# Low parts of the output weights made twice, rows kept on chip through the MLP, sums spread, casts ahead

## The chip, the core and the metric

The kernel runs on one core of one Trainium2 chip. The metric is the device time of one execution in microseconds (us), the median of three runs. In what follows PE is the matrix engine, VectorE is DVE in the views, ScalarE is ACT, GpSimd is POOL, and SP is the engine that issues most transfers.

## What is computed

One layer on 2048 rows of 1024 features: a mixer, a cross attention to 256 memory tokens, and an MLP, each added to the running rows `h`.

```python
h = h + jnp.concatenate([y_pool, y_dn], axis=-1) @ w_out[l]
m = rmsnorm(mem, mem_norm_g[l])
h = h + memory_cross_attention(rmsnorm(h, norm_xattn_g[l]), m, w_xq[l], w_xk[l], w_xv[l], w_xo[l])
h = h + sqrelu_mlp(rmsnorm(h, norm_mlp_g[l]), w_up[l], w_down[l])
return rmsnorm(h, final_norm_g)          # sqrelu: relu(h w_up) squared, times w_down
```

The result of `rmsnorm` is a row times one factor r = 1/sqrt(mean(h^2) + eps) times a gain. The squared relu makes r come out of the MLP as r^2.

## The kernel before

After a prologue (the mixer and the memory's keys and values, up to about 873 us) the rest is 22 products of 1024 x 1024 blocks, called macros here and numbered 0 to 21. Macros 0 and 1 are the output projection (`o`) of the first and the second half of the rows (`sb` 0 and 1), 2 and 3 the scores (`s`), 4 and 5 the values (`v`), and 6 to 21 are up (`u`) and down (`d`) of the MLP in four groups of columns, the first half in 6 to 13, the second in 14 to 21.

A macro is done with seven block products instead of eight, its steps idx 0 to 6. Each step is 48 matmuls of 128 x 512 on PE (line 1003): each operand is split in a high part (cast by ScalarE, `sh`, `th`) and a low part (what is left, by VectorE, `sl`, `tl`), and three of the four products are taken. `S` is the operand with rows, `T` the weight side. Both need sums and differences of blocks: `adds` makes those of `S`, and `sums` makes those of `T` in eight units per matrix, each fetched by two transfers on GpSimd's queue into a tile `cb_...`, worked on by four additions (lines 161 to 164) on VectorE up to macro 6 and on GpSimd after it, and stored to `sums_...` by a transfer on GpSimd's queue. SP's queue loads them later as `t`.

In the first half's `o`, `s` and `v` macros each low part `tl` is also stored to `lo_o`, `lo_s`, `lo_v`, and the second half loads it from there on GpSimd's queue (line 929, in `prep`) instead of making it again.

The rows `or`, `sr`, `vr`, `dr` take the results: VectorE adds each 128 x 512 result to them (line 1037; for scores line 1055 with the row maximum, then exponentials on ScalarE, line 1066, and the scaling, lines 1071 and 1075). The first half's rows lie in eight tiles of the pool `h`, the second half's in eight of the ten of the pool `a`. `squares` takes the sums of squares and stores rows to `h_d`; after `v` it also scales the rows by r in place (line 1102), so that `turned` can transpose them on PE (line 1115, 64 transposes per macro, in steps 0, 2 and 3 of macros 1 to 6). The down macro's rows `dr` are loaded again from `h_d`.

PE's order is written out by hand throughout. For steps up to the end of macro 6 so are those of ScalarE, VectorE and GpSimd (`step_fixed`); from macro 7 on (`step_free`) a scheduler sets those. Each engine and each queue works in order: what waits holds all that is behind it.

## Time and profile before

| | |
|---|---|
| median of three runs | 2756.51 us (2750.58 to 2762.46) |
| the profiled execution | 2760.52 us |
| its span | 2758.6 us |
| PE busy | 2581.2 us, 94% of the span |
| VectorE busy | 1946.4 us, 71% |
| ScalarE busy | 1383.2 us, 50% |
| GpSimd busy | 836.3 us, 30% |
| moved by DMA | 518.65 MB |

[...]

### The profile page before, as it was taken

What the parts mean: (1) busy time and instruction counts of PE and PEld (TensorE: products, weight loads), DVE (VectorE), ACT (ScalarE), POOL (GpSimd) and SP (SyncE); (2) the same over time, 40 slices, a digit from 0 to 9 for tenths busy, and PEclk for the clock granted to TensorE, in tenths of its full rate; (3) what the DMA queues carried; (4) which work ended last, traced back from release to release, by engine and by line L of the source; (5) the groups of instructions that cost most, each with busy time, mean ns of one, the idle gap of its engine ahead of it and who ended that gap; (6) DMA issues with size and microseconds to landing.
All of it is one profiled execution on the core that took longest, in us unless ns stands there. A gap on an engine that the chain in (4) does not pass through costs nothing.

```text
span 2758.6 us, 35256 instructions
## 1 busy us (share of the span) xinstructions
PE 2581.2 (94%) x12822; PEld 2163.5 (78%) x12822; DVE 1946.4 (71%) x2531; ACT 1383.2 (50%) x2290; POOL 836.3 (30%) x881
## 2 busy tenths in 40 slices
PE   7999999999998987988997889999999999999998
PEld 6887788789787766776785678788888788888887
DVE  6865776765775766667657687888768685767666
ACT  6436535635534344675444435445464645545463
POOL 4333454431432222000012377887111202021100
PEclk9999999999999999999998999999999999999999
DMA  4335255244238999767998866656344634333232
GB/s 141 93 104 189 69 176 184 76 123 138 72 108 271 380 383 333 277 229 275 357 336 305 287 212 225 220 186 242 107 153 142 225 99 144 108 120 132 92 99 107
DMA packets 257080, 518.65 MB, mean 188 GB/s; under 512 B 36150, under 2 KB 106379, under 8 KB 256907
## 3 DMA queue, kind: packets, MB, share of 16 engines
q1 hardware_dynamic: 192858, 397.90, 42.8%
q0 software_dynamic: 28064, 97.53, 10.2%
q10 hardware_dynamic: 35984, 20.98, 2.7%
q8 instruction: 100, 1.64, 0.2%
q14 instruction: 74, 0.60, 0.1%
HBM read 383.17 MB, written 133.17 MB: 187 GB/s over the span
## 4 chain that ended last, share of the span: by engine, by line
PE 49%; DVE 12%; DMA 8%; issue 7%; ACT 5%; POOL 2%; SPq 0%; DVEq 0%; POOLq 0%; ACTq 0%
PE A L1003 23%; PE B L1003 17%; DVE tl L91 2%; DMA sums_v<-cb_v 2%; DVE sl L91 1%; DMA sums_w<-cb_w 1%; DMA or<-in_x_dram 1%; PE pcm L98 1%; PE pcm L99 1%; PE pcm L97 1%; ACT sh L90 1%; DVE cac L379 1%; ACT sr L1066 1%; PE px L492 1%; DMA t<-in_w_out_dram 1%
## 5 line engine op out<-in xcount | busy, mean ns | idle before, releaser
L1003 PE MATMUL A<-tl,sh 128*128 128x512 f32 x1392 | 549.0, 394 | 24.3 <-DMA tl<-lo_o 20.6
L1003 PE MATMUL A<-th,sh 128*128 128x512 f32 x1392 | 551.9, 396 | 12.4 <-DVE dr L1037 8.8
L1003 PE MATMUL A<-th,sl 128*128 128x512 f32 x1392 | 547.5, 393 | 0.0
L1003 PE MATMUL B<-tl,sh 128*128 128x512 f32 x1056 | 418.7, 397 | 26.3 <-DVE tl L91 9.3
L1003 PE MATMUL B<-th,sh 128*128 128x512 f32 x1056 | 418.4, 396 | 22.2 <-DVE nrs L1127 7.9
L1003 PE MATMUL B<-th,sl 128*128 128x512 f32 x1056 | 416.8, 395 | 0.0
L91 DVE TENSOR_TENSOR tl<-t,th 128x1024 fp32r<-128x1024 f32 x264 | 379.4, 1437 | 3.8 <-ACT th L90 3.6
L91 DVE TENSOR_TENSOR sl<-x,sh 128x1024 fp32r<-128x1024 f32 x166 | 225.5, 1359 | 184.4 <-ACT sh L90 184.0
L1003 PEld LDWEIGHTS A<-tl,sh 128*128 128x128 f32 x1392 | 265.2, 191 | 82.6 <-DMA tl<-lo_o 21.4
L1003 PEld LDWEIGHTS A<-th,sh 128*128 128x128 f32 x1392 | 265.1, 190 | 68.4 <-issue 9.6
L1003 PEld LDWEIGHTS A<-th,sl 128*128 128x128 f32 x1392 | 264.7, 190 | 55.5
L90 ACT CAST th<-t 128x1024 fp32r<-128x1024 f32 x264 | 275.7, 1044 | 36.2 <-DMA t<-sums_w 16.9
L90 ACT CAST sh<-x 128x1024 fp32r<-128x1024 f32 x166 | 173.8, 1047 | 221.1 <-PE B L1003 110.8
L1003 PEld LDWEIGHTS B<-tl,sh 128*128 128x128 f32 x1056 | 202.1, 191 | 73.5 <-DVE tl L91 12.7
L1003 PEld LDWEIGHTS B<-th,sh 128*128 128x128 f32 x1056 | 202.2, 191 | 66.4 <-ACT th L90 8.6
L1003 PEld LDWEIGHTS B<-th,sl 128*128 128x128 f32 x1056 | 202.0, 191 | 42.1
L90 ACT CAST sh<-c 128x1024 fp32r<-128x1024 f32 x96 | 100.3, 1045 | 218.8 <-PE A L1003 115.4
L97 PE MATMUL pcm<-hhi_x,wh_in 128*128 128x512 f32 x512 | 208.2, 407 | 0.2 <-ACT wh_in L90 0.2
L99 PE MATMUL pcm<-hhi_x,wl_in 128*128 128x512 f32 x512 | 205.1, 402 | 2.3 <-DVE wl_in L91 2.3
L98 PE MATMUL pcm<-hlo_x,wh_in 128*128 128x512 f32 x512 | 204.3, 399 | 0.0
L91 DVE TENSOR_TENSOR sl<-c,sh 128x1024 fp32r<-128x1024 f32 x96 | 126.8, 1321 | 65.4 <-ACT sh L90 65.4
L379 DVE SCALAR_TENSOR_TENSOR cac<-raw,vec,cac 128x512 f32<-128x512 f32 x144 | 129.3, 898 | 2.3
(359 smaller groups left out, 4720.8 us busy)
## 6 DMA issues: line engine op xcount, KB each, us to landing
ws_in<-in_w_in_dram SPq DMA_DIRECT2D x72, 512.0 KB, 3.8
x<-in_w_up_dram SPq DMA_DIRECT2D x64, 512.0 KB, 5.4
t<-sums_n SPq DMA_DIRECT2D x64, 512.0 KB, 4.5
t<-sums_w SPq DMA_DIRECT2D x64, 512.0 KB, 3.3
t<-n_d SPq DMA_DIRECT2D x48, 512.0 KB, 4.3
t<-in_w_down_dram SPq DMA_DIRECT2D x48, 512.0 KB, 4.9
cb_w<-in_w_down_dram POOLq DMA_DIRECT2D x64, 256.0 KB, 5.5
sums_w<-cb_w POOLq DMA_DIRECT2D x32, 512.0 KB, 4.2
```

The lines of the kernel that those rows point to most:

```text
L90: nc.scalar.copy(hi, ps)
L91: nc.vector.tensor_tensor(lo, ps, hi.bitcast(F32), ALU.subtract)
L97: nc.tensor.matmul(ps, lhsT=lh, rhs=rh, start=first, stop=False)
L98: nc.tensor.matmul(ps, lhsT=lh, rhs=rl, start=False, stop=False)
L99: nc.tensor.matmul(ps, lhsT=ll, rhs=rh, start=False, stop=last)
L379: nc.vector.scalar_tensor_tensor(a5, raw[:, j:j + 512], g_cv[:, j, ch:ch + 1], a5, ALU.mult, ALU.add)
L492: nc.tensor.matmul(px[:, h * P:(h + 1) * P], lhsT=vT[:, h, :], rhs=cur[:, h, :], start=True, stop=True)
L1003: nc.tensor.matmul(ps, lhsT=l_[:, a0:a0 + P], rhs=r_[:, b0:b0 + TB], start=start and c == 0 and i_ == 0, stop=last and c == 3 and i_ == 2, ...
L1066: nc.scalar.activation(pv[:, i, :], sv[:, i, :], AF.Exp, bias=mx[:, i:i + 1], scale=rs[:, t:t + 1], accum_out=sx[:, i:i + 1])
```

## The change

- `lo_o` is gone: macro 1 makes its 14 low parts `tl` on VectorE, as macro 0 does. `lo_s` and `lo_v` stay.
- The first half's `v` rows are neither scaled nor stored: the down macros add to them where they lie. `squares` makes r^2 (`rv`, by an addition and a reciprocal on VectorE) instead of r, and the down addition becomes a `scalar_tensor_tensor` that multiplies the result by r^2 and adds the row. The second half's rows are still stored and loaded again, without the scaling.
- The units of `sums` get other places: those of `s` start in step 1 of macro 0 with up to three fetched ahead, `v` is done half in macro 1 and half in macro 3, `w0` half in macro 2 and half in macro 6, `n0` in macro 5 with two fetched ahead. Those of `n0` move from the pool `h` to `a` and `wx`.
- `prep` issues the casts of `S` and `T` on ScalarE together, and VectorE's low parts after the additions of results; exponentials, scalings, evictions of transposes and squares take other places in a step.

```diff
-    lo_d = {key: dram.tile([7, 2, P, D], F32, tag=f"lo_{key}", name=f"lo_{key}") for key in "osv"}
+    lo_d = {key: dram.tile([7, 2, P, D], F32, tag=f"lo_{key}", name=f"lo_{key}") for key in "sv"}
...
-        nxt = fetch(0)
+        ready = []
+
+        def fill(u, n, end):
+            while len(ready) < n and u + len(ready) < end:
+                ready.append(fetch(u + len(ready)))
+
         for u, (c, h) in enumerate(units):
-            t_ = nxt
-            if u + 1 < len(units):
-                nxt = fetch(u + 1)
+            end = len(units) if u >= stop else stop
+            fill(u, depth, end)
+            t_ = ready.pop(0)
+            fill(u + 1, depth, end)
...
-        known = kind in "osv" and sb > 0
+        known = kind in "sv" and sb > 0
         for i in range(2):
             T.append([wtile(w_, a, f"{a}_{nm}_{i}", F32R) for a in ("th", "tl")])
             if known:
                 nc.gpsimd.dma_start(T[i][1].bitcast(F32), lo_d[kind][LO[j], i])
         for i in range(2):
             S.append([wtile(w_, a, f"{a}_{nm}_{i}", F32R) for a in ("sh", "sl")])
-            split_ps(*S[i], raw[i])
+            nc.scalar.copy(S[i][0], raw[i])
+            nc.scalar.copy(T[i][0], m["T"][j][i])
             yield
-            if known:
-                nc.scalar.copy(T[i][0], m["T"][j][i])
-            else:
-                split_ps(*T[i], m["T"][j][i])
-                if kind in "osv":
+            nc.vector.tensor_tensor(S[i][1], raw[i], S[i][0].bitcast(F32), ALU.subtract)
+            if not known:
+                nc.vector.tensor_tensor(T[i][1], m["T"][j][i], T[i][0].bitcast(F32), ALU.subtract)
+                if kind in "sv":
...
+            if kind == "d" and g == 0 and sb == 0:
+                cur[kind, sb] = cur["v", sb]
+            elif kind in "osv" or (kind == "d" and g == 0):
...
-        nc.vector.tensor_tensor(h_[:, sl], ps, h_[:, sl], ALU.add)
+        if kind == "d":
+            nc.vector.scalar_tensor_tensor(h_[:, sl], ps, rowsc["v", sb, r // 4][:, t:t + 1], h_[:, sl],
+                                           ALU.mult, ALU.add)
+        else:
+            nc.vector.tensor_tensor(h_[:, sl], ps, h_[:, sl], ALU.add)
...
-            nc.sync.dma_start(h_d[sb][(4 * half + t) * P:(4 * half + t + 1) * P, :], h_)
+            if kind == "o" or sb > 0:
+                nc.sync.dma_start(h_d[sb][(4 * half + t) * P:(4 * half + t + 1) * P, :], h_)
...
-        rs = sm.tile([P, 4], F32, tag="rs4", name=f"rs{kind}{sb}_{half}", bufs=2)
-        powmh(rs, ss, EPS)
+        if kind == "o":
+            rs = sm.tile([P, 4], F32, tag="rs4", name=f"rs{kind}{sb}_{half}", bufs=2)
+            powmh(rs, ss, EPS)
+        else:
+            rowsc["v", sb, half] = rs = sm.tile([P, 4], F32, tag="rv", name=f"rv{sb}_{half}", bufs=4)
+            nc.vector.tensor_scalar_add(rs, ss, EPS)
...
-            for t, h_ in enumerate(hs):
-                nc.vector.tensor_scalar_mul(h_, h_, rs[:, t:t + 1])
+            nc.vector.reciprocal(rs, rs)
...
+    dense = (4, 4, 4, 5, 5, 5, 6, 6)
+    late = (3, 3, 4, 4, 5, 5, 6, 6)
     full = (2, 2, 3, 3, 4, 4, 5, 5)
-    late = (3, 3, 4, 4, 5, 5, 6, 6)
-    for k, i, where in (("s", 0, full), ("v", 1, full), ("n0", 5, (4, 4, 4, 5, 5, 5, 6, 6)), ("w0", 6, late),
-                        ("w1", 7, full), ("n1", 8, late), ("w2", 9, full), ("w3", 11, full)):
-        alloc = {0: lambda nm: wtile(ap_, "a", nm), 5: lambda nm: wtile(hpl, "h", nm)}
-        alloc = alloc.get(max(i - 1, 0) if i < 2 else i, lambda nm: wtile(wx, "wn", nm))
-        for idx in where:
-            plan.setdefault((i, idx), []).append((k, alloc))
-    gens = {}
-
-    def sum_units(i, idx, half=None):
+    for k, where in (("s", [(0, i) for i in (1, 2, 2, 3, 3, 4, 4, 5)]),
+                     ("v", [(b, i) for b in (1, 3) for i in (3, 4, 5, 6)]),
+                     ("w0", [(2, i) for i in (1, 3, 4, 5)] + [(6, i) for i in (3, 4, 5, 6)]),
+                     ("n0", [(5, i) for i in dense]), ("w1", [(7, i) for i in full]),
+                     ("n1", [(8, i) for i in late]), ("w2", [(9, i) for i in full]), ("w3", [(11, i) for i in full])):
+        for at in where:
+            plan.setdefault(at, []).append(k)
+    gens, now = {}, [0]
+
+    def side_tile(nm):
+        if now[0] < NA and not (nm[:5] == "cb_n0" and nm[-1] in "135"):
+            return wtile(ap_, "a", nm)
+        return wtile(wx, "wn", nm)
...
+            done, exps, scal = outs[:], second[:], then[:]
+            outs[:] = []
+            after(done)
+            second[:] = after(held)
+            held[:] = []
+            then[:] = after(exps)
+            if t < 2:
                 next(pr, None)
-            done = outs[:]
-            outs[:] = []
-            if t < 2:
-                after(done)
-            second = after(held)
-            held[:] = []
+            after(scal)
             if t == 1:
                 for _ in pr:
                     pass
@@ -1187,37 +1212,33 @@
                     next(sq[k - 1, 1])
                 if normed and idx == 1:
                     next(sq[k - 1, 0])
-                if 0 < idx < 3:
-                    adds(k, idx + 1)
-            third = after(second)
-            if t > 1:
-                after(done)
-            after(then)
-            then[:] = third
+            if t == 2 and 0 < idx < 3:
+                adds(k, idx + 1)
```

GpSimd's queue, behind macro 6. `sums_w0` of `cb_w0_7` is the store of the last unit for the first down macro, `cb_w1_...` are the units for the second. Before:

```order
L146 DMA cb_w0_7_14388<-in_w_down_dram 128x2x256 x2
L165 DMA sums_w0_100<-cb_w0_6_14333 128x4x256
L146 DMA cb_w1_0_14615<-in_w_down_dram 128x2x256 x2
L165 DMA sums_w0_100<-cb_w0_7_14388 128x4x256
L161 TENSOR_TENSOR cb_w1_0_14615<-cb_w1_0_14615 128x256
...
L164 TENSOR_TENSOR cb_w1_0_14615<-cb_w1_0_14615 128x256
L165 DMA sums_w1_101<-cb_w1_0_14615 128x4x256
L146 DMA cb_w1_1_14618<-in_w_down_dram 128x2x256 x2
```

And now:

```order
L171 DMA sums_w0_99<-cb_w0_6_14201 128x4x256
L146 DMA cb_w1_0_14560<-in_w_down_dram 128x2x256 x2
L167 TENSOR_TENSOR cb_w1_0_14560<-cb_w1_0_14560 128x256
...
L170 TENSOR_TENSOR cb_w1_0_14560<-cb_w1_0_14560 128x256
L171 DMA sums_w1_100<-cb_w1_0_14560 128x4x256
L146 DMA cb_w1_1_14563<-in_w_down_dram 128x2x256 x2
L167 TENSOR_TENSOR cb_w1_1_14563<-cb_w1_1_14563 128x256
...
L170 TENSOR_TENSOR cb_w1_1_14563<-cb_w1_1_14563 128x256
L171 DMA sums_w1_100<-cb_w1_1_14563 128x4x256
L171 DMA sums_w0_99<-cb_w0_7_14286 128x4x256
```

The store of `cb_w0_7` stood behind the fetch of `cb_w1_0`; now it stands behind two whole units of `w1`.

GpSimd's queue in macro 1, where the loads of `lo_o` stood between the units of `v`. Before:

```order
L929 DMA tl_11_0_10081<-lo_o_92 128x1024
...
L146 DMA cb_v_3_10142<-vwo_d_81 128x2x256 x2
L165 DMA sums_v_97<-cb_v_2_10056 128x4x256
L146 DMA cb_v_4_10182<-vwo_d_81 128x2x256 x2
L165 DMA sums_v_97<-cb_v_3_10142 128x4x256
L929 DMA tl_12_0_10211<-lo_o_92 128x1024
L929 DMA tl_12_1_10214<-lo_o_92 128x1024
```

And now, with the four units that are left in macro 1:

```order
L146 DMA cb_v_0_10140<-vwo_d_81 128x2x256 x2
L146 DMA cb_v_1_10143<-vwo_d_81 128x2x256 x2
L171 DMA sums_v_96<-cb_v_0_10140 128x4x256
L146 DMA cb_v_2_10227<-vwo_d_81 128x2x256 x2
L171 DMA sums_v_96<-cb_v_1_10143 128x4x256
L146 DMA cb_v_3_10323<-vwo_d_81 128x2x256 x2
L171 DMA sums_v_96<-cb_v_2_10227 128x4x256
L103 TENSOR_TENSOR rso1_1_10428<-rso1_1_10428,mhalf_110 128x4
L171 DMA sums_v_96<-cb_v_3_10323 128x4x256
L103 TENSOR_TENSOR rso1_0_10532<-rso1_0_10532,mhalf_110 128x4
```

The loads are gone from between the stores, and half of the units went to macro 3.

VectorE at the start of macro 4, where the last scores are still turned into weights. Before:

```order
L91 TENSOR_TENSOR sl_29_0_12182<-x12_29_0_12034,sh_29_0_12181 128x1024
L91 TENSOR_TENSOR tl_29_0_12178<-t_29_0_12042,th_29_0_12177 128x1024
L1055 TENSOR_TENSOR sr1_3_11100<-B25_3_11812,sr1_3_11100 128x512
L1059 TENSOR_REDUCE mx27_3_12189<-sr1_3_11100 128x2
L1061 TENSOR_SCALAR mx27_3_12189<-mx27_3_12189,rw1_1_0_10673 128x2
L1070 RECIPROCAL sx27_2_12147<-sx27_2_12147 128x2
L1075 TENSOR_SCALAR sr1_2_11099<-sr1_2_11099,sx27_2_12147 128x256
L91 TENSOR_TENSOR sl_29_1_12211<-x12_29_1_12036,sh_29_1_12210 128x1024
...
L1037 TENSOR_TENSOR vr0_0_11917<-A28_0_12161,vr0_0_11917 128x512
...
L1075 TENSOR_SCALAR sr1_3_11100<-sr1_3_11100,sx27_3_12192 128x256
...
L1127 COPY nrs1_1_1_12260<-pts1_1_1_12239 128x512
```

And now:

```order
L1065 TENSOR_TENSOR sr1_3_11074<-B25_3_11808,sr1_3_11074 128x512
L1069 TENSOR_REDUCE mx27_3_12197<-sr1_3_11074 128x2
L1071 TENSOR_SCALAR mx27_3_12197<-mx27_3_12197,rw1_1_0_10626 128x2
L939 TENSOR_TENSOR sl_29_0_12193<-x12_29_0_12040,sh_29_0_12192 128x1024
L941 TENSOR_TENSOR tl_29_0_12189<-t_29_0_12048,th_29_0_12188 128x1024
...
L1047 TENSOR_TENSOR vr0_0_11915<-A28_0_12172,vr0_0_11915 128x512
L939 TENSOR_TENSOR sl_29_1_12222<-x12_29_1_12042,sh_29_1_12221 128x1024
...
L1080 RECIPROCAL sx27_2_12200<-sx27_2_12200 128x2
L1085 TENSOR_SCALAR sr1_2_11073<-sr1_2_11073,sx27_2_12200 128x256
...
L1141 COPY nrs1_1_1_12276<-pts1_1_1_12256 128x512
```

The addition of the last score tile (`sr1_3`) now stands ahead of the low parts of step 29, and the scaling of `sr1_2` behind all four of them.

## Rows read from the trace of the kernel before

**Rows 1.** Windows, macros 0 to 9: stretch, length, busy us, clock, DMA share, GB/s.

```profile
873.10:962.80 89.70, 83.31 (x353) 67.28 (x353) 66.75 (x93) 37.92 (x58) 22.63 (x33) 0.94 1.01 376
962.80:1084.00 121.20, 90.04 (x402) 72.77 (x401) 68.70 (x104) 45.60 (x61) 29.62 (x42) 0.89 0.96 358
1084.00:1173.10 89.10, 85.58 (x401) 70.63 (x400) 61.96 (x91) 61.84 (x120) 3.27 (x5) 0.98 0.83 295
1173.10:1270.10 97.00, 89.00 (x402) 72.61 (x401) 60.03 (x103) 68.45 (x141) 5.83 (x11) 0.95 0.79 280
1270.10:1368.00 97.90, 87.18 (x401) 71.52 (x400) 73.42 (x95) 44.57 (x68) 2.67 (x4) 0.93 0.80 281
1368.00:1468.80 100.80, 89.57 (x402) 73.30 (x401) 59.56 (x84) 40.03 (x50) 22.43 (x34) 0.92 0.97 350
1468.80:1578.00 109.20, 90.77 (x402) 72.45 (x400) 75.11 (x98) 56.55 (x74) 24.92 (x26) 0.91 0.81 284
1578.00:1666.80 88.80, 79.45 (x338) 63.55 (x337) 76.81 (x79) 33.00 (x34) 63.13 (x63) 0.98 0.65 216
1666.80:1742.90 76.10, 76.10 (x337) 63.04 (x336) 59.18 (x40) 44.96 (x54) 63.59 (x54) 1.00 0.72 241
1742.90:1825.40 82.50, 79.43 (x337) 65.00 (x336) 67.28 (x65) 32.35 (x34) 66.48 (x66) 0.96 0.65 209
```

**Rows 2.** Waits of PE in macro 1: us in total, times, longest.

```profile
PE A L1003 <- DMA tl<-lo_o: 20.6, 2, 12.7
PE B L1003 <- DMA tl<-lo_o: 9.0, 3, 7.4
```

**Rows 3.** Waits of PE in macros 2 to 4.

```profile
PE B L1003 <- DVE nrs L1127: 7.9, 1, 7.9
PE B L1003 <- ACT sr L1071: 4.9, 1, 4.9
```

**Rows 4.** Waits of PE in macros 5 and 6.

```profile
PE ptv L1115 <- DVE vr L1102: 12.6, 8, 8.7
PE B L1003 <- DMA tl<-lo_v: 8.0, 1, 8.0
```

**Rows 5.** Waits of PE from macro 7 to the end.

```profile
PE A L1003 <- DVE dr L1037: 8.8, 2, 5.7
```

**Rows 6.** Groups of DVE by form, macro 1: busy us, mean ns | idle before.

```profile
L91 DVE TENSOR_TENSOR sl<-x,sh 128x1024 fp32r<-128x1024 f32 x14 | 17.0, 1218 | 1.6 <-ACT sh L90 1.5
...
L161 DVE TENSOR_TENSOR cb_v<-cb_v 128x256 f32<-128x256 f32 x8 | 3.4, 424 | 28.3 <-DMA cb_v<-vwo_d 28.3
```

**Rows 7.** Groups of DVE by form, whole span.

```profile
L1037 DVE TENSOR_TENSOR dr<-A,dr 128x512 f32<-128x512 f32 x128 | 85.7, 684 | 32.2 <-PE A L1003 30.6
...
L1043 DVE SCALAR_TENSOR_TENSOR dr<-dr,rs_f,gf 128x512 f32<-128x512 f32 x32 | 26.7, 882 | 9.4 <-POOL rs_f L103 9.4
L94 DVE SCALAR_TENSOR_TENSOR hlo_x<-ptr_x,g_mix,hhi_x 128x512 fp32r<-128x512 f32 x32 | 23.2, 748 | 15.8 <-ACT hhi_x L93 15.5
...
L1102 DVE TENSOR_SCALAR vr<-vr,rsv 128x1024 f32<-128x1024 f32 x16 | 11.2, 748 | 2.7 <-DMA h_d<-vr 2.7
...
L611 DVE SCALAR_TENSOR_TENSOR po<-pl,rawu 128x512 f32<-128x512 f32 x16 | 11.0, 685 | 26.1 <-POOL pl L608 26.1
```

**Rows 8.** Timeline of POOL behind macro 6: start, us, engine, line.

```profile
1591.88 0.78 POOL L165 DMA_DIRECT2D sums_w<-cb_w  x1 [0.27 <-DVE cb_w L164]
1593.48 1.56 POOL L161 TENSOR_TENSOR cb_w<-cb_w 128x256 f32<-128x256 f32 x1 [0.82 <-DMA cb_w<-in_w_down_dram]
...
1606.23 0.78 POOL L161 TENSOR_TENSOR cb_w<-cb_w 128x256 f32<-128x256 f32 x1 [0.67 <-DMA cb_w<-in_w_down_dram]
```

**Rows 9.** DMA issues on the page: xcount, KB each, us to landing.

```profile
t<-sums_w SPq DMA_DIRECT2D x64, 512.0 KB, 3.3
...
cb_w<-in_w_down_dram POOLq DMA_DIRECT2D x64, 256.0 KB, 5.5
sums_w<-cb_w POOLq DMA_DIRECT2D x32, 512.0 KB, 4.2
```

More of the change, by code (lines that the diff above doesn't have):

```diff
@@ L134, in y_quad, with sums @@
         return y_half(key, kh)[:, nh * TB:(nh + 1) * TB]
-    def sums(key, alloc, eng):
+    def sums(key, alloc, eng, depth, stop):
         W = TB // 2
@@ L846, in prep_first @@
                     split_ps(first[hi][c // 2][:, sl], first[lo][c // 2][:, sl], raw)
-                if c % 2 == 1:
-                    nc.sync.dma_start(lo_d["o"][0, c // 2], first["tl"][c // 2].bitcast(F32))
                 yield
@@ L975, in open_rows @@
             kind, sb, g = macros[k]
-            if kind in "osv" or (kind == "d" and g == 0):
+            if kind == "d" and g == 0 and sb == 0:
+                cur[kind, sb] = cur["v", sb]
+            elif kind in "osv" or (kind == "d" and g == 0):
                 cur[kind, sb] = rows(kind, sb)
@@ L1135, in hymba_layer, with sum_units @@
     plan = {}
+    dense = (4, 4, 4, 5, 5, 5, 6, 6)
+    late = (3, 3, 4, 4, 5, 5, 6, 6)
     full = (2, 2, 3, 3, 4, 4, 5, 5)
-    late = (3, 3, 4, 4, 5, 5, 6, 6)
-    for k, i, where in (("s", 0, full), ("v", 1, full), ("n0", 5, (4, 4, 4, 5, 5, 5, 6, 6)), ("w0", 6, late),
-                        ("w1", 7, full), ("n1", 8, late), ("w2", 9, full), ("w3", 11, full)):
-        alloc = {0: lambda nm: wtile(ap_, "a", nm), 5: lambda nm: wtile(hpl, "h", nm)}
-        alloc = alloc.get(max(i - 1, 0) if i < 2 else i, lambda nm: wtile(wx, "wn", nm))
-        for idx in where:
-            plan.setdefault((i, idx), []).append((k, alloc))
-    gens = {}
-    def sum_units(i, idx, half=None):
+    for k, where in (("s", [(0, i) for i in (1, 2, 2, 3, 3, 4, 4, 5)]),
[10 more added lines that the diff above has]
+        return wtile(wx, "wn", nm)
+    def sum_units(i, idx, t=None):
         todo = plan.get((i, idx), ())
-        if half is not None:
-            todo = todo[:1] if half == 0 else todo[1:]
-        for k, alloc in todo:
+        now[0] = i
+        if t is not None:
+            todo = todo[max(t - 4 + len(todo), 0):max(t - 3 + len(todo), 0)]
+        for k in todo:
             if k not in gens:
-                gens[k] = sums(k, alloc, nc.vector if i <= NA else nc.gpsimd)
+                gens[k] = sums(k, side_tile, nc.vector if i <= NA else nc.gpsimd, {"s": 3, "n0": 2}.get(k, 1),
+                               4 if k in ("v", "w0") else 0)
             next(gens[k])
     held, sq, tu = [], {}, {}
-    then, outs = [], []
+    second, then, outs = [], [], []
     def after(fs):
@@ L1165, in step_fixed @@
         loads(n + 2)
-        if idx == 5 and (k < NA or k == NA):
+        if idx == 5:
             open_rows(k + 1)
@@ L1200, in step_fixed @@
             if k < NA and mc[0] != "s" and idx == 6:
-                if t == 1:
+                if t == 2:
                     sq[k, 1] = squares(mc[0], mc[1], 1)
-                if t in (1, 2):
+                if t in (2, 3):
                     next(sq[k, 1])
@@ L1209, in step_fixed @@
                     next(sq[k - 1, 0])
-            if idx == 6 and k < NA and t % 2 == 1:
-                adds(k + 1, t // 2)
-            if t % 2 == 1:
-                sum_units(k, idx, t // 2)
+            if idx == 6 and k < NA and t > 1:
+                adds(k + 1, t - 2)
+            sum_units(k, idx, t)
     def close_fixed():
-        second = after(held)
-        third = after(second)
+        for _ in range(4):
+            then_, exps = then[:], second[:]
+            second[:] = after(held)
+            held[:] = []
+            then[:] = after(exps)
+            after(then_)
         after(outs)
-        after(then)
-        after(third)
     def step_free(n):
```

## The prediction

> **What bounds the kernel now.** I read three views in turn: the windows by macro, PE's waits macro by macro, and VectorE's groups. The reader should see in the first that a macro in which nothing is late takes 76.1 us: macro 8, clock 1.00, PE busy for all of it [rows 1]. So PE's own order is the bound, and only what makes PE late can be won. Macros 1 to 6 also hold 64 transposes each. Macro 2's busy time of 85.6 us, at a clock of 0.98, is the most that matmuls and transposes together can need [rows 1]; I take 84.
>
> The length of each macro over 76.1 (over 84 for 1 to 6) is then what waiting costs, the slow clock behind each wait included [rows 1]: 13.6 us in macro 0, and 37.2, 5.1, 13.0, 13.9, 16.8 and 25.2 in macros 1 to 6, together 124.8. Macro 7 has 12.7, macro 9 has 6.4. The rest of the second half of the trace the change leaves alone but for the down additions.
>
> The waits give the causes. In macro 1 PE waits 20.6 + 9.0 = 29.6 us for `tl` from `lo_o` [rows 2]. The remaining 7.6 of its 37.2 go with a clock of 0.89, so a wait costs about a quarter more than its length. In macros 2 to 4 the long ones are 7.9 us for an eviction of transposes on VectorE and 4.9 us for a scaling on ScalarE [rows 3]: two engines that work in order and take turns. In macros 5 and 6 they are 12.6 us for the scaling of `vr`, and 8.0 us for `tl` from `lo_v` [rows 4].
>
> **Part 1, lo_o.** 14 stores and 14 loads of 512 KB go, 7.3 MB in macro 0 and 7.3 in macro 1. The 29.6 us and their clock go with them. VectorE gets 14 low parts at 1.218 us, the row of the same operation there [rows 6], 17.1 us. Four units of `v` leave the macro: sixteen operations at 0.424 us [rows 6], 6.8 us. Its load rises from 68.7 to 79.0 of some 92 us. PE now needs `tl` from an engine that is busy for nearly nine tenths of the time, and I leave 8 us of waiting. Macro 0 moved 376 GB/s at a DMA share of 1.01 [rows 1] and loses its stores, but its units come earlier: 12 instead of 13.6.
>
> **Part 2, rows kept.** 16 scalings go, 11.2 us of VectorE's time, with the 12.6 us that PE waits for them [rows 4, 7]. So do 8.4 MB of stores and loads about macros 5 and 6, of 35.3 MB that macro 5 moves (350 GB/s for 100.8 us) [rows 1]. The price is the new form of the down addition, 28 in each of eight down macros, 224 in all. An addition takes 0.684 us now. The nearest row to the new form, a result in PSUM with a factor per row and a second operand, is 0.748 [rows 7]. The bounds are 0.685 (the same operation without a factor per row) and 0.882 (all operands in SBUF) [rows 7]. I take 0.748: 0.064 each, 1.8 us per macro, 14.3 in all. PE hides that where VectorE has room; it shows only where PE waited for these additions, 8.8 us in macros 7 and 9 [rows 5]. I add 0.6 to macro 9 and take macro 7's into the boundary below. At 0.882 it would be 5.5 us per macro, at most 11 in these two; at 0.685 nothing.
>
> [...]
>
> **Part 3, sums spread.** Four units of `w0` go from macro 6 to macro 2 and four of `v` from macro 1 to macro 3, 6.8 us of VectorE and 4.2 MB each time. Macro 2 then has 68.8 us of VectorE work, macro 3 66.8, below macro 4's 73.4 [rows 1]; macro 3's transfers rise from 27.2 to 31.4 MB in some 90 us, about 350 GB/s, macro 5's rate. But loads of `lo_s` now stand behind units' stores in macro 3, as loads of `lo_v` still do in macro 5, and a store waits for VectorE. I leave 5 us in macro 2, 6 in macro 3, 7 in macro 5.
>
> The boundary of macros 6 and 7 is where time is given back. The last store of `w0` stood behind the fetch of one unit of `w1`; it now stands behind two units with their stores, as the order shows. The second unit's fetch needs the buffer that the first one's store frees. Count from the start of macro 6's last step, when the seventh unit of `w0` is stored: 4.2 us until it lands, two issues of 0.8 and 5.5 for the fetch, four additions of 0.78 to 1.56, 0.8 and 4.2 for the store, 1.6 and 5.5 for the second fetch, four additions, 1.6 for two stores' issue, 4.2 to land, 3.3 to load [rows 8, 9]. That sums to 38.7 to 44.9 us; cast and low part add 2.4, both taken at the low part's 1.218 [rows 6]. PE wants the tile three steps (76.1/7 = 10.9 each) and half of a chain of 2.7 on, at 34. It waits some 7 to 13 us, 10 taken, half of it again for the clock and the additions that then stand behind on VectorE (before, PE's longest wait for these was 5.7 [rows 5]), and 4 for what was late there besides. I put macro 7 at 19 for 12.7.
>
> **Part 4, casts ahead.** Additions of results now stand ahead of low parts, and both casts are made before either low part is asked for, as the order shows for macro 4. The 7.9 and 4.9 us [rows 3] and their clock go. I leave 5 us in macro 4 and 6 in macro 6, whose 25.2 also held most of part 2's waits. On SP's queue first loads of the next macro now stand between the stores of evicted transposes; those stores wait for their evictions, so these loads can come some us later, which is in the 5 to 7 us left per macro. Late next is whatever VectorE issues last in a step, the low parts.
>
> **Sum.** Macros 0 to 6 keep 12 + 8 + 5 + 6 + 5 + 7 + 6 = 49 of 124.8: 75.8 us won. Macro 7 gives back 6.3 and macro 9 0.6. That is 68.9 us, 2691.6 against the profiled 2760.5. The median is 4.0 us under the profiled execution, so I predict 2688.
>
> **Rivals.**
> - The waits go whole. If the last store of `w0` leaves early enough (macro 7 at 8) and macros 1 to 6 keep 4 us each, 24 for 37, the time is 2688 - 11 - 13 = 2664. For it: macro 8 runs without a wait at 241 GB/s and 59 us of VectorE [rows 1]. Against: queues in order behind three engines seldom leave nothing.
> - The waits move. VectorE is asked for more in macros 1 to 3, and every macro of 1 to 6 goes as macro 4 did, 13.9 [rows 1]: 83 for 37, 2688 + 46 = 2734. For it: macro 4 had 73.4 us of VectorE work and no load from `lo_`. Against: its long wait was of the turn-taking that part 4 undoes.
> - Slower than before. VectorE becomes what PE waits for in every step of macros 1 to 6, as in macro 6, where it had 75.1 us of work and the excess was 25.2 [rows 1]: 151 for 37, 2688 + 114 = 2802. It decides from 18 us per macro, 2.5 per step. For it: macro 1's 79.0. Against: macros 2, 3 and 6 stay below 70, and macro 6's waits were mostly for the scaling that goes.
> [...]
>
> **Chances.** The forecast 0.53, whole waits 0.20, moved waits 0.17, slower 0.07, half rate 0.03. A change under 0.5%, 14 us, is about what can't be told from none. Faster by more than that is under 2743: the first two, half rate, and 0.11 of the moved waits, 0.87. Within is the rest of the moved waits, 0.06; slower 0.07. The likeliest one's own range is 2670 to 2710. For 8 in 10 the range goes to 2652, where the waits vanish and the boundary costs no more than macro 9's 6.4, and to 2740, past the moved waits.
>
> **What would show it.** Right: no PE wait on `lo_o` or on a scaling of `vr`; macro 1 at 92 us and macros 2 to 6 near 90; PE waiting at the third step of macro 7 for a `tl` whose `t` comes from `sums_w`; the new addition at 0.75 us; macros 10 to 21 as before. Wrong: PE's waits for VectorE's low parts in macros 1 to 3 of over 10 us each, a macro 7 near 80, or down macros that grow by 6.

## The result, and the profile after

The changed kernel takes 2679.5 us (2678.14 to 2686.13, four runs) against 2757.48 (2750.58 to 2762.46, four runs): a ratio of 0.9724, interval 0.9697 to 0.9751. The profiled execution took 2678.6 us, with a span of 2676.9. The forecast was 2688, from 2691.6 for the profiled execution.

The windows by macro come first, as in [rows 1]. They show macros 0 to 9, then 11 and 14. The columns are the stretch, its length, the busy time of PE, PE's weight loads, VectorE, ScalarE and GpSimd, the granted clock, the DMA share and GB/s.

```profile
873.20:962.50 89.30, 83.96 (x352) 68.00 (x353) 76.55 (x106) 39.87 (x60) 23.33 (x34) 0.94 0.97 355
962.50:1045.80 83.30, 83.30 (x401) 69.69 (x400) 71.02 (x91) 43.61 (x59) 12.08 (x14) 1.00 0.91 331
1045.80:1130.20 84.40, 83.55 (x401) 69.62 (x400) 69.59 (x115) 65.96 (x128) 12.26 (x17) 1.00 0.94 339
1130.20:1217.70 87.50, 84.85 (x402) 69.44 (x401) 64.19 (x113) 65.40 (x136) 13.95 (x22) 1.00 0.91 335
1217.70:1309.10 91.40, 84.84 (x401) 70.67 (x400) 70.63 (x94) 43.42 (x64) 2.39 (x4) 0.96 0.92 325
1309.10:1407.90 98.80, 86.64 (x401) 71.65 (x400) 60.16 (x86) 41.91 (x53) 21.94 (x33) 0.93 0.93 333
1407.90:1495.60 87.70, 85.17 (x401) 70.86 (x400) 64.39 (x82) 57.15 (x73) 18.99 (x21) 0.98 0.81 286
1495.60:1581.60 86.00, 79.10 (x338) 64.43 (x337) 69.55 (x68) 29.79 (x31) 57.74 (x56) 0.96 0.55 182
1581.60:1657.70 76.10, 76.10 (x337) 63.03 (x336) 51.39 (x40) 46.54 (x56) 56.46 (x55) 1.00 0.74 251
1657.70:1733.90 76.20, 76.20 (x338) 63.08 (x337) 66.06 (x65) 30.71 (x32) 60.44 (x58) 1.00 0.63 207
1810.00:1894.80 84.80, 79.22 (x338) 65.01 (x338) 71.59 (x64) 29.62 (x31) 30.97 (x23) 0.96 0.37 120
2047.10:2133.80 86.70, 79.82 (x337) 64.68 (x336) 60.19 (x53) 51.29 (x67) 20.55 (x10) 0.94 0.60 206
```

Macro 1 fell from 121.2 to 83.3 us. PE is busy for all of it at a clock of 1.00, so 83.3 is what matmuls and transposes together need there. Before, PE waited 12.65 us in this macro for one `tl`, and behind that wait eight matmuls started 0.43 us apart at a granted clock of 0.50, against 0.23 us apart at 1.00. Macros 0 to 6 take 622.4 us instead of 704.9. Macro 7 is 2.8 us shorter and macro 9 6.3 us shorter. Macros 11 and 14 grew by 6.0 (from 78.8) and 3.7 (from 83.0). The balance is 82.5 + 2.8 + 6.3 - 6.0 - 3.7 = 81.9 us, the difference of the two profiled executions (2760.5 and 2678.6).

PE's waits answer to [rows 2 to 5]. The fence has the long ones of macros 3, 4, 5 and 6 and all of macro 7's but one of 0.4: us in total, times, longest.

```profile
PE B L1009 <- DMA tl<-lo_s: 1.6, 2, 0.9
...
PE B L1009 <- ACT nrs L1137: 6.6, 1, 6.6
...
PE B L1009 <- DMA tl<-lo_v: 10.5, 1, 10.5
...
PE B L1009 <- DVE nrv L1143: 2.5, 1, 2.5
...
PE A L1009 <- DVE vr L1044: 5.8, 1, 5.8
PE A L1009 <- DVE tl L941: 0.8, 1, 0.8
```

The waits for `lo_o` and for the scaling of `vr` are gone. The one for `lo_v` in macro 5 grew from 8.0 [rows 4] to 10.5. A wait for an eviction of transposes stays in macro 4: 6.6 us, now on ScalarE, for 7.9 on VectorE before [rows 3]. Macro 1 has no wait of PE.

VectorE's groups over the whole span, as [rows 7]: form and count, busy us, mean ns, idle before.

```profile
L1044 DVE SCALAR_TENSOR_TENSOR dr<-A,rv,dr 128x512 f32<-128x512 f32 x64 | 46.8, 748 | 15.8 <-PE A L1009 15.8
L1044 DVE SCALAR_TENSOR_TENSOR vr<-A,rv,vr 128x512 f32<-128x512 f32 x64 | 46.2, 742 | 12.8 <-PE A L1009 12.8
...
L1053 DVE SCALAR_TENSOR_TENSOR vr<-vr,rs_f,gf 128x512 f32<-128x512 f32 x16 | 17.5, 1142 | 2.7 <-POOL rs_f L103 2.7
```

The new form of the down addition takes 0.742 to 0.748 us, for which 0.748 had been taken. The third row, with a mean of 1.142, is explained below.

### The profile page after: what moved, and what is told of

Same layout as the page of the kernel before. It is cut to its first block, busy times and chain, and to the rows that moved or that the text cites. A ratio compares the mean times of both kernels' runs of the same rounds, so it can differ in the third digit from the quotient of the medians.

```text
span 2676.9 us, 35124 instructions
## 1 busy us (share of the span) xinstructions
PE 2558.5 (96%) x12822; PEld 2153.5 (80%) x12822; DVE 1949.6 (73%) x2537; ACT 1383.3 (52%) x2286; POOL 812.7 (30%) x863
## 4 chain that ended last, share of the span: by engine, by line
PE 59%; DVE 8%; DMA 6%; ACT 4%; issue 4%; POOL 2%; POOLq 0%; DVEq 0%; SPq 0%; ACTq 0%
PE A L1009 28%; PE B L1009 21%; DMA t<-vwo_d 1%; DVE tl L941 1%; PE pcm L98 1%; PE pcm L99 1%; PE pcm L97 1%; DVE sl L939 1%; DMA sums_w<-cb_w 1%; DVE cac L385 1%; PE px L498 1%; DMA sums_n<-cb_n 1%; ACT sh L936 1%; DMA cb_n<-n_d 1%; DVE xb L466 1%
## 5 line engine op out<-in xcount | busy, mean ns | idle before, releaser
L1009 PE MATMUL B<-tl,sh 128*128 128x512 f32 x1056 | 416.3, 394 | 21.5 <-DMA tl<-lo_v 10.5
L1009 PE MATMUL B<-th,sh 128*128 128x512 f32 x1056 | 415.7, 394 | 12.6 <-ACT nrs L1137 6.6
L941 DVE TENSOR_TENSOR tl<-t,th 128x1024 fp32r<-128x1024 f32 x278 | 391.1, 1407 | 12.1 <-ACT th L937 12.1
L937 ACT CAST th<-t 128x1024 fp32r<-128x1024 f32 x306 | 320.6, 1048 | 49.2 <-DMA t<-sums_w 19.1
L939 DVE TENSOR_TENSOR sl<-x,sh 128x1024 fp32r<-128x1024 f32 x166 | 218.5, 1316 | 121.4 <-ACT sh L936 121.4
L936 ACT CAST sh<-c 128x1024 fp32r<-128x1024 f32 x96 | 100.8, 1050 | 226.6 <-PE A L1009 121.2
```

Source lines behind the costliest of these rows:

```text
L936: nc.scalar.copy(S[i][0], raw[i])
L937: nc.scalar.copy(T[i][0], m["T"][j][i])
L939: nc.vector.tensor_tensor(S[i][1], raw[i], S[i][0].bitcast(F32), ALU.subtract)
L941: nc.vector.tensor_tensor(T[i][1], m["T"][j][i], T[i][0].bitcast(F32), ALU.subtract)
L1009: nc.tensor.matmul(ps, lhsT=l_[:, a0:a0 + P], rhs=r_[:, b0:b0 + TB], start=start and c == 0 and i_ == 0, stop=last and c == 3 and i_ == 2, ...
```

## The experiments

Each kernel is the changed one with the edit shown, or, from e9 on, the kernel that is named with it. The diffs are cut. A time stands beside the changed kernel's 2679.5; e10 and e11 had five runs each, the others one. A single time is good to a few us: the changed kernel's own four span 8.0 (2678.14 to 2686.13), and the prologue, which no edit but e1's touches, ends between 869.4 and 873.5 us in the others. So the macros' lengths carry the argument. The table gives the length of each macro in us, from its first matmul to the next one's, for the macros that differ.

| macro | after | e1 | e2 | e4 | e5 | e3 | e6 | e7 | e8 | e9 | e10 | e11 | e11b |
|---|---|---|---|---|---|---|---|---|---|---|---|---|---|
| 1 | 83.3 | 96.8 | 83.3 | 83.4 | 102.5 | 83.4 | 83.4 | 83.4 | 83.3 | 83.4 | 83.3 | 83.3 | 83.4 |
| 2 | 84.4 | 84.4 | 84.4 | 88.3 | 87.3 | 84.4 | 84.4 | 84.4 | 84.4 | 84.4 | 84.4 | 84.4 | 84.4 |
| 3 | 87.5 | 88.2 | 87.4 | 99.1 | 84.6 | 87.6 | 87.4 | 90.8 | 87.5 | 87.6 | 88.0 | 88.3 | 88.5 |
| 4 | 91.5 | 92.7 | 92.4 | 97.8 | 88.4 | 92.3 | 92.8 | 93.3 | 92.8 | 92.1 | 86.9 | 86.4 | 88.5 |
| 5 | 98.8 | 94.0 | 97.1 | 96.8 | 99.4 | 97.5 | 83.3 | 96.5 | 98.1 | 83.3 | 83.3 | 83.3 | 83.8 |
| 6 | 87.7 | 93.3 | 95.8 | 90.6 | 96.7 | 90.8 | 98.8 | 90.9 | 90.0 | 97.8 | 100.1 | 94.2 | 98.5 |
| 7 | 85.9 | 89.8 | 89.9 | 85.9 | 90.9 | 88.1 | 91.4 | 76.4 | 85.9 | 88.3 | 76.4 | 76.3 | 76.4 |
| 9 | 76.2 | 77.8 | 76.2 | 76.6 | 77.8 | 77.6 | 77.4 | 76.2 | 76.5 | 78.0 | 80.0 | 80.2 | 76.2 |
| 10 | 76.2 | 76.2 | 76.2 | 81.7 | 82.7 | 76.2 | 76.2 | 76.5 | 81.8 | 76.2 | 76.2 | 76.2 | 76.5 |
| 11 | 84.7 | 80.7 | 83.6 | 83.3 | 83.7 | 80.9 | 80.9 | 84.3 | 82.4 | 81.4 | 82.5 | 81.7 | 84.3 |
| 14 | 86.7 | 86.0 | 86.0 | 86.4 | 86.3 | 83.3 | 86.7 | 86.5 | 86.7 | 86.0 | 87.3 | 85.8 | 86.0 |

**e1: `lo_o` back (part 1 undone).**

```diff
...
-        known = kind in "sv" and sb > 0
+        known = kind in "osv" and sb > 0
...
-                if kind in "sv":
+                if kind in "osv":
```

> Part 1 alone is undone: macro 0 stores its low parts to lo_o again and macro 1 loads them on GpSimd's queue; units, casts and rows stay as changed. Theory A (the loads are late because they stand behind units' stores on GpSimd's queue, whatever VectorE does): macro 1 goes from 83 us back to 105 to 120, PE's waits on lo_o are 15 us or more, all other macros stay within 2 us, the whole is 2700 to 2716. Rival B (the waits of macro 1 left with the four units that moved to macro 3 and with the casts, and making the low parts again was not needed): macro 1 stays under 92, the whole under 2690.

2700.82 us. Macro 1 has 96.8, 13.5 more, between what the two theories had. PE's waits in macro 1:

```profile
PE A L1011 <- DMA tl<-lo_o: 3.5, 2, 3.2
PE B L1011 <- DVE nro L1145: 3.3, 1, 3.3
PE pto L1131 <- DVE or L1049: 1.4, 1, 1.4
```

With the units in their new places the loads of `lo_o` hold PE for 3.5 us, not for 29.6 [rows 2]: much of what bears `lo_o`'s name before goes with the units around its loads, or with the order within a step, which e1 also leaves as changed; the two aren't told apart. The first theory's 15 us of waits on `lo_o` didn't come, nor did the rest hold still: macros 6 and 7 lose 9.5 as well and macro 5 wins 4.8, though nothing there was edited.

**e5: old places of the units (part 3 undone, but for `n0`).**

```diff
-    for k, where in (("s", [(0, i) for i in (1, 2, 2, 3, 3, 4, 4, 5)]),
-                     ("v", [(b, i) for b in (1, 3) for i in (3, 4, 5, 6)]),
-                     ("w0", [(2, i) for i in (1, 3, 4, 5)] + [(6, i) for i in (3, 4, 5, 6)]),
+    for k, where in (("s", [(0, i) for i in full]),
+                     ("v", [(1, i) for i in full]),
+                     ("w0", [(6, i) for i in late]),
...
-                gens[k] = sums(k, side_tile, nc.vector if i <= NA else nc.gpsimd, {"s": 3, "n0": 2}.get(k, 1),
-                               4 if k in ("v", "w0") else 0)
+                gens[k] = sums(k, side_tile, nc.vector if i <= NA else nc.gpsimd, {"n0": 2}.get(k, 1), 0)
```

> Part 3 alone is undone but for n0 (whose tiles must stay out of the kept rows' pool): s units in steps 2 to 5 of macro 0 with one fetch ahead, all v units in macro 1, all w0 units in macro 6. Theory A (the spread made room on VectorE in macros 1 and 6, which else are full): macro 1 grows by 3 to 10 us since its VectorE load goes to 86 us, macro 6 with 7 by 5 to 12 as the units pile up in the last step, the whole is 2687 to 2702. Rival B (VectorE had room, and the spread only moves units and their transfers): under 3 us in either place, the whole within 4 us of 2679.

2713.02 us, the dearest part by itself, and dearer than expected. In macro 1 PE now waits for VectorE's own low parts:

```profile
PE A L1009 <- DVE tl L941: 6.9, 3, 4.4
PE B L1009 <- DVE tl L941: 4.7, 2, 3.8
```

VectorE has 79.0 us of work there, for 71.0 in the changed kernel, and waits for fetches of units itself:

```profile
DVE cb_v L167 <- DMA cb_v<-vwo_d: 17.4, 3, 6.8
```

A unit's additions stand ahead of the low parts in VectorE's order, so a late fetch reaches PE through `tl`. Macro 1 is 19.2 longer, where 3 to 10 were expected. Macro 1 reaches 83.3 only with parts 1 and 3 both: of the 37.9 us by which it fell, e1 gives 13.5 back and e5 19.2.

**e2: the scalings back, by ones (part 2 in part).**

```diff
+            for t, h_ in enumerate(hs):
+                nc.vector.tensor_scalar_mul(h_, h_, ones[:, 0:1])
```

> The 16 scalings of the v rows on VectorE are put back at their old place, as multiplications by 1.0 from a column of ones; rows stay on chip and the factor stays in the down additions, so nothing is left out. Theory A (PE waited for these in-place scalings because the transposes read the rows): PE waits 8 to 13 us for them in macros 5 and 6 together, 16 operations of 0.75 us, the whole grows by 9 to 18 to 2688 to 2697. Rival B (with casts ahead and additions first VectorE now reaches them in time): under 4 us of waits, the whole under 2684.

2684.74 us. The wait comes back, 9.7 us in macro 6 and 1.3 in macro 5, together near the 12.6 of before [rows 4]:

```profile
PE ptv L1131 <- DVE vr L1118: 9.7, 4, 9.2
```

Macros 6 and 7 are 8.1 and 4.0 longer, but the whole only 5 to 6, between the two theories: macro 5 is 1.7 shorter, macros 11 and 14 together 1.8, and the prologue ends 2.4 us sooner. The stores and loads of these rows weren't put back, so their share of part 2 isn't measured.

**e4: the old order within a step (part 4 undone).** The diff turns the order within a step back to that of the kernel before: casts with their low parts, results added behind them.

```diff
-            nc.scalar.copy(S[i][0], raw[i])
-            nc.scalar.copy(T[i][0], m["T"][j][i])
+            split_ps(*S[i], raw[i])
...
-            second[:] = after(held)
-            held[:] = []
-            then[:] = after(exps)
```

> Part 4 alone is undone: within a step of macros 0 to 6 casts, low parts, additions, exponentials, scalings, evictions of transposes, squares and adds stand in the old order; units, lo_o and rows stay as changed. Theory A (VectorE and ScalarE waiting for each other in turn made the waits of macros 2 to 4): macros 2 to 4 grow by 12 to 22 us together, macro 6 by 2 to 8, the whole is 2693 to 2710. Rival B (these waits came from the transfers and units about them, and went with lo_o and the spreading): macros 2 to 4 grow by under 5, the whole under 2686.

2703.57 us. Macros 2 to 4 have 21.8 more, and the waits of [rows 3] are back in nearly their old sizes:

```profile
PE B L1009 <- DVE nrs L1141: 7.6, 1, 7.6
PE B L1009 <- ACT sr L1081: 4.9, 1, 4.9
PE pts L1129 <- DVE sr L1065: 3.7, 2, 3.5
```

So the order within a step was the cause of these, with one rest: macro 4's eviction keeps PE waiting for 6.6 us in the changed kernel, on the other engine.

**e3: the plain addition.** This kernel leaves out the factor r^2 of the down additions.

```diff
-        if kind == "d":
-            nc.vector.scalar_tensor_tensor(h_[:, sl], ps, rowsc["v", sb, r // 4][:, t:t + 1], h_[:, sl],
-                                           ALU.mult, ALU.add)
-        else:
-            nc.vector.tensor_tensor(h_[:, sl], ps, h_[:, sl], ALU.add)
+        nc.vector.tensor_tensor(h_[:, sl], ps, h_[:, sl], ALU.add)
```

> The down additions are plain additions again: the factor r^2 per row is left out of the MLP's part, all else is as changed. Theory A (the new form costs VectorE 0.06 us each and PE nearly nothing): additions of 0.68 us for 0.74, macros 7 and 11 shorter by 0.3 to 1.5 us each, others unchanged, the whole 2676 to 2680. Rival B (the new form is what made macro 11 grow from 78.8 to 84.7 us and macro 14 from 83.0 to 86.7): macro 11 back under 80.5, the whole 2668 to 2674.

2676.38 us, 3 less, as the first theory had it, but not where it had it: macro 7 is 2.2 longer. The price of the new form lies in macro 14, 83.3 as before the change (83.0); the twelve kernels with the new form have 85.8 to 87.3 there. Macro 11 is 3.8 shorter too, but e1 and e6, which keep the new form, have 80.7 and 80.9 there, so that isn't the form's.

**e7: one unit of `w0` earlier.**

```diff
-                     ("w0", [(2, i) for i in (1, 3, 4, 5)] + [(6, i) for i in (3, 4, 5, 6)]),
+                     ("w0", [(2, i) for i in (1, 3, 4, 5, 6)] + [(6, i) for i in (3, 4, 5)]),
...
-                               4 if k in ("v", "w0") else 0)
+                               {"v": 4, "w0": 5}.get(k, 0))
```

> Five units of w0 are done in macro 2 (the fifth in its last step) and three in macro 6, the last of them in its fifth-last sum place, step index 5, so that the last store of w0 is issued about 11 us earlier and no whole unit of w1 stands before it. Theory A (macro 7's 9.8 us over the floor come from that store: the weights of step 2 land late, VectorE idles for them and then does its adds in front of the additions PE waits for): macro 7 falls from 85.9 to 76 to 79, the whole to 2669 to 2674. Rival B (VectorE's adds in step 2 beside GpSimd's units alone do it, as in macro 11, which has 84.7 with its units stored in time): macro 7 stays over 82.

2671.42 us. Macro 7 takes 76.4 instead of 85.9, and no wait of PE is left in it. The late store of the last unit of `w0` was the cause of what macro 7 kept. Macros 3 and 6 are 3.3 and 3.2 longer; in macro 3 the fifth unit in macro 2's last step is the likely reason, which isn't shown.

**e8: VectorE's additions of down macros in later steps.**

```diff
...
-        elif idx == 1:
+        elif idx == 1 and mc[0] == "u":
...
+        elif idx in (2, 4) and mc[0] == "d":
+            adds(k, 2 + idx // 4)
```

> In down macros the two groups of adds on VectorE that stand in step index 1 move to steps 2 and 4; all else is as changed. Theory A (in macro 11 four adds of 128x1024 on VectorE, slowed to about 1.8 us each while GpSimd adds too, stand in front of the additions that free PE's accumulators): macro 11 falls from 84.7 to 76 to 80, macro 7 by 2 to 6, the whole to 2668 to 2675. Rival B (what is late there is the weights' load, since ScalarE waited for t): macro 11 stays over 83.

2684.17 us. Macro 11 falls by only 2.3, macro 7 not at all, and macro 10 grows by 5.6: the theory fell. At 82.4, macro 11 doesn't bear out the rival either.

**e6: the last step's low parts of `v` made again instead of stored and loaded.**

```diff
-        known = kind in "sv" and sb > 0
+        known = kind in "sv" and sb > 0 and (kind, j) != ("v", 3)
...
-                if kind in "sv":
+                if kind in "sv" and sb == 0 and (kind, j) != ("v", 3):
```

> For the last step of macro 5 alone the low parts of the weights are made on VectorE (2 more operations of 1.22 us) instead of loaded from lo_v, and macro 4 doesn't store them; so no load stands behind the n0 units on GpSimd's queue. Theory A (PE waits 10.5 us there for a load that is issued late and lands in 11 us): macro 5 falls from 98.8 to 84 to 89, the whole to 2664 to 2672. Rival B (the weights' load t of that step is as late, as all transfers crowd there): macro 5 stays over 94.

2678.58 us. Macro 5 runs at its 83.3, 15.5 less, as expected; and all of it is given back, 11.1 in macro 6 and 5.5 in macro 7. VectorE's waits in macro 6:

```profile
DVE n L957 <- DMA sums_n<-cb_n: 6.0, 1, 6.0
```

An addition at the start of macro 6 wants a tile that the store of a sum still reads.

**e9: e6, and that addition one step later.**

```diff
+            if k == NA and idx == 1 and t == 0:
+                after(outs)
+                outs[:] = []
+                adds(k, 1)
...
-            if idx == 6 and k < NA and t > 1:
+            if idx == 6 and k < NA and (t == 2 or t == 3 and k < NA - 1):
```

> As the run that makes the last low parts of macro 5 on VectorE, and the adds of macro 6 that need a tile of wx (the n adds) move from the last step of macro 5 to the start of step 1 of macro 6. Theory A (the 15.5 us won in macro 5 were given back at the start of macro 6, because the second n add waited 6.0 us for the store of an n0 unit to free its tile, with the additions and evictions behind it in VectorE's order): macro 6 falls from 98.8 to 84 to 90, macro 5 stays at 83 to 85, the whole is 2660 to 2670. Rival B (n0's units fetch and store too late there whatever waits behind them): macro 6 stays over 94.

2669.25 us, but macro 6 keeps 97.8: the rival. (Of the 9.3 us less than e6, 5.1 lie in the prologue and macro 0, which weren't edited.) ScalarE's waits in macro 6 show the next in line:

```profile
ACT c L1022 <- DMA sums_n<-cb_n: 7.9, 1, 7.9
```

A copy of a result waits for the store of such a sum too. Behind it on ScalarE stand the squares, VectorE waits 2.9 us for these (`rv`), and its evictions come behind that; PE waits 7.3 us for `nrv`. VectorE's eviction also waits 4.4 us for the store of an earlier `nrv`, so this chain is only one candidate until e11.

**e10: the three moves together**: e9, one unit of `w0` earlier, and three units of `v` in macro 3 instead of four.

```diff
-                     ("v", [(b, i) for b in (1, 3) for i in (3, 4, 5, 6)]),
-                     ("w0", [(2, i) for i in (1, 3, 4, 5)] + [(6, i) for i in (3, 4, 5, 6)]),
+                     ("v", [(1, i) for i in (2, 3, 4, 5, 6)] + [(3, i) for i in (3, 4, 5)]),
+                     ("w0", [(2, i) for i in (1, 2, 3, 4, 5)] + [(6, i) for i in (3, 4, 5)]),
...
-                               4 if k in ("v", "w0") else 0)
+                               5 if k in ("v", "w0") else 0)
```

> All that the runs so far point to, together: the last low parts of macro 5 made on VectorE, the n adds of macro 6 in its step 1, w0 with five units in steps 1 to 5 of macro 2 and three in steps 3 to 5 of macro 6, v with five units in steps 2 to 6 of macro 1 and three in steps 3 to 5 of macro 3. Theory A (these waits are independent): macro 1 83 to 87, macros 3 and 4 together 172 to 178 (now 179), macro 5 83 to 85, macro 6 84 to 90, macro 7 76 to 79, the whole 2646 to 2660. Rival B (a wait taken away in one macro comes back in the next, as macro 5's did): 2662 or more.

2663.76 us (2657.09 to 2669.58), a ratio of 0.9656, interval 0.9637 to 0.9675. Macros 4, 5 and 7 gain 29.6 and macro 6 takes 12.4 of it back: the rival.

**e11: e10, with ScalarE's copies held over the first step of macro 6.**

```diff
-            second[:] = after(held)
-            held[:] = []
+            second[:] = []
+            if k < NA or idx > 0 or t == 0:
+                second[:] = after(held)
+                held[:] = []
```

> The version with three steps spread anew (w0's units earlier, v's last sums stored in macro 4, the n additions at step 1), and now also with the copies of results that fall due at the first step of macro 6 held until its second step. Theory A: macro 6's 100.1 us come from ScalarE, whose copy waits some 7.8 us for the store of a sum to free its tile, with the squares behind it, VectorE's r^2 behind these and the evictions of transposes behind that; with the copy held, macro 6 falls to 84-92 us, and the whole from 2664 to 2645-2656. Rival B: the wait is for the transfers themselves and turns up elsewhere (at the second step of macro 6, or in macro 7): macro 6 or 7 longer by what is won, 2660 or more.

2653.82 us (2650.59 to 2655.05), a ratio of 0.9611, interval 0.9589 to 0.9633, below the changed kernel's whole interval. This version beats both kernels. Macro 6 in it:

```profile
1386.00:1480.20 94.20, 86.40 (x401) 71.01 (x401) 73.68 (x89) 58.92 (x76) 23.74 (x25) 0.96 0.85 302
```

Macro 6 falls from 100.1 to 94.2. That wins 5.9 of the 12.4 that e10 gave back there, a little less than expected. PE still waits there for the eviction:

```profile
PE B L1009 <- DVE nrv L1143: 4.3, 1, 4.3
```

**e11b: e11 without the moved addition.**

```diff
-            if k == NA and idx == 1 and t == 0:
-                after(outs)
-                outs[:] = []
-                adds(k, 1)
...
-            if idx == 6 and k < NA and (t == 2 or t == 3 and k < NA - 1):
+            if idx == 6 and k < NA and t > 1:
```

> The same as the version with the held copies, but the n additions of macro 6 back at step 0. Theory A (the copy on ScalarE is what held the evictions, the additions hardly): macro 6 within 3 us of the version with both held. Rival B (VectorE's addition waits for the same stored sum, about 6 us, as in the run that moved v's sums alone): macro 6 longer by 4-8 us.

2660.32 us, and macro 6 has 98.5, 4.3 more, with the addition's wait back at 5.7 us. So both instructions that wanted a tile held PE up, the copy for 5.9 us and the addition for 4.3. Moved alone, with the copy still waiting, the addition won only 1.0 (e6 to e9). What keeps the rest of macro 6's 94.2 above 83.3 is open.

## Why the prediction was right

The direction, the mechanism and most of the size held. The profiled execution came out 13.0 us under the sum: macros 0 to 6 gave 6.7 more than forecast, macro 7 9.1 more and macro 9 6.9 more, and macros 11 and 14, which had been left as they were, took 6.0 and 3.7. That it came so near is in part luck, since the terms miss both ways: macros 1 to 3 came 15.8 us under theirs, macro 5 7.8 over.

Of the signs set down for being right, three came: no wait on `lo_o` or on a scaling of `vr`, a wait at the third step of macro 7 (though of only 0.8 us), and 0.75 us for the new addition. Macro 1 at 92, macros 2 to 6 near 90 (84.4 to 98.8) and macros 10 to 21 as before did not come. One sign of being wrong did: a down macro, 11, grew by 6. The new form alone isn't why, since e1 and e6 keep it and have 80.7 and 80.9 there.

- **Part 1 with part 3, macro 1.** Forecast 92, measured 83.3. VectorE has 71.0 us of work there, not the 79.0 that were added up, and macro 0, whose work was not counted, rose from 66.8 [rows 1] to 76.6. The 8 us left for waiting were too cautious. Before, VectorE waited 28.3 us there for fetches of `v` [rows 6]; now it waits for PE alone. e5, where it waits for fetches again, has 79.0 us of work as well, so it doesn't tell the load from the fetches.
- **Macros 2 and 3.** Forecast 89 and 90, measured 84.4 and 87.5. 0.7 us per macro is the floor, 83.3 instead of 84.
- **Part 4, macros 2 to 4.** Here half of the step failed. Macro 3's 4.9 us for a scaling went, as forecast. Macro 4's wait for an eviction did not: 7.9 us on VectorE became 6.6 on ScalarE, and macro 4 kept 91.4 for a forecast of 89. e4 brings both old waits back, and macro 4 to 97.8. The rest goes with `v`'s units in macro 3: macro 4 takes 86.9 in e10, with three there for four, and 88.4 in e5, with none; PE's wait falls to 3.4 and 3.2. No run moves these units alone.
- **Part 2.** The scaling's 12.6 us went, and e2 brings 11.0 of it back. The new addition's 0.748 was right; 0.882, the upper bound, was no price at all. That row [rows 7] mixes 30 instructions of about 0.75 with two of 2.88 and 2.90. In the rows of one line (min, median and max ns), the kernel before and then the changed kernel:

```profile
L1043 DVE SCALAR_TENSOR_TENSOR dr<-dr,rs_f,gf x32: 737/748/2899, 2118.6 to 2754.1; 128x512 f32<-128x512 f32 x32
```

```profile
L1053 DVE SCALAR_TENSOR_TENSOR vr<-vr,rs_f,gf x16: 735/746/2890, 2033.1 to 2065.7; 128x512 f32<-128x512 f32 x16
```

  A mean was read as the cost of a form. No run shows the half rate that has 0.03 among the chances: the new form (one source in PSUM) has means of 0.742 and 0.748 us, the second row (both in SBUF) a median of 0.746, and a plain addition has 0.684 [rows 7].
- **Macro 5 was missed.** 7 us were left over 84, and it kept 14.8. GpSimd's queue shows it: start, duration, instruction, and the idle time before it.

```profile
1380.89 1.42 POOL L146 DMA_DIRECT2D cb_n<-n_d  x2 [3.98 <-DMA sums_n<-cb_n]
1382.31 0.77 POOL L171 DMA_DIRECT2D sums_n<-cb_n  x1
1383.07 1.08 POOL L933 DMA_DIRECT2D tl<-lo_v  x2
```

  The load of `lo_v` stands behind fetches that wait for stores. It was issued at 1383.07, PE wanted it at 1383.9 and had it at 1394.37. That is late issue and slow landing: this pair took 11.3 and 12.6 us to land, against a median of 6.6 of the twelve loads of `lo_v` before it, by which PE would have had it at 1389.7, an estimate.

```profile
DMA to landing us min/median/max: 11.3/11.9/12.6
```

```profile
DMA to landing us min/median/max: 3.6/6.6/8.5
```

  The prediction had seen this queue ("as loads of `lo_v` still do in macro 5") and gave it too little. e6 takes the load away, and macro 5 falls to 83.3; it doesn't tell late issue from slow landing.
- **The boundary of macros 6 and 7.** 19 forecast, 9.8 measured, with the mechanism as described (e7). The queue in the new trace:

```profile
1482.29 0.78 POOL L171 DMA_DIRECT2D sums_w<-cb_w  x1
1488.76 1.42 POOL L146 DMA_DIRECT2D cb_w<-in_w_down_dram  x2 [5.69 <-DMA sums_w<-cb_w]
...
1496.70 0.77 POOL L171 DMA_DIRECT2D sums_w<-cb_w  x1 [0.30 <-POOL cb_w L170]
1500.36 1.41 POOL L146 DMA_DIRECT2D cb_w<-in_w_down_dram  x2 [2.88 <-DMA sums_w<-cb_w]
...
1509.03 1.53 POOL L171 DMA_DIRECT2D sums_w<-cb_w  x2 [0.30 <-POOL cb_w L170]
```

  From the seventh unit's store to the end of the eighth's issue it takes 28.3 us (1510.56 - 1482.29); the working had 31.2 to 37.4 up to there (38.7 to 44.9 less 4.2 and 3.3). A fetch is back within 3.3 us of its issue, and 5.5 had been taken from the page's median over the whole program. PE waited 0.8 us for the tile itself (and 0.4 for its cast), not 10. The 5.8 us came from VectorE, where the tile's low part was followed by four additions of `c` and by low parts, ahead of the evictions into `vr` that PE wanted; that had been forecast, clock included, at half of the 10:

```profile
1520.39 2.89 DVE L960 TENSOR_TENSOR c<-n,c 128x1024 f32<-128x1024 f32 x2
1523.20 2.89 DVE L963 TENSOR_TENSOR c<-c,n 128x1024 f32<-128x1024 f32 x2
...
1535.02 2.05 DVE L1044 SCALAR_TENSOR_TENSOR vr<-A,rv,vr 128x512 f32<-128x512 f32 x3
```

- **Macros 9, 11 and 14.** Macro 9 was to keep its 6.4 and 0.6 more, and kept none: PE's 3.1 us there for an addition went. No run shows why. Its code is the same in the changed kernel and all experiments but e3 and e8, and it takes 76.2 to 80.2 us in these. For 11 and 14 the step "the rest of the second half of the trace the change leaves alone but for the down additions" failed. What the trace has on these two is in the last section; for macro 11 the cause stays open.

The result lies in the likeliest case's own range (2670 to 2710), towards the whole waits' 2664. That rival had macro 7 at 8 over 76.1, which is nearly what came (9.8), but macro 5's 14.8 kept it off.

## What to carry to other kernels

A transfer that waits in an in-order queue behind the store of an earlier sum is late by that store (macro 7 kept 9.8 us, and e7 wins 9.5 of them back); look for what holds a buffer before you count bytes. The name on a wait need not be what to change: loads of `lo_o` held PE for 29.6 us before and for 3.5 in e1. And a part undone alone has the price that the others leave it: e1, e2, e4 and e5 cost 21.3 + 5.2 + 24.1 + 33.5 = 84.1 us of a gain of 78.0, though e2 and e5 undo theirs only in part. What one stage wins (15.5 in e6) the next can lose whole, so follow a gain through the stages behind it. And take the median of a form, not its mean, as its price.
